# The residual of a decoder layer kept in its own column order, normalised in place, with the memory of a staging ring as a place of the weight stream

## The chip, the cores and the metric

The kernel runs on one core of a Trainium2 chip, as one launch. The metric is the device time of the execution in microseconds (us). The kernel before was run three times: 1680.66, 1681.29 and 1682.52 us, with a median of 1681.29.

## The reference, cut to what matters

One layer of a decoder with 256 tokens of 2048 channels, all in float32. Three attention branches are projected, gated and merged; then comes the part that the change touches, and a mixture of 32 experts:

```python
x = layer_norm(ALPHA * x + merged @ w_o, ln1_g, ln1_b)      # 256 x 2048
y = hier_moe(x, w_grp, b_grp, w_rt, b_rt, w1, w3, w2)
x = layer_norm(ALPHA * x + y, ln2_g, ln2_b)
# hier_moe: logits for 4 groups and 32 experts, best group, best two experts inside it;
#   hid = silu(xt @ w1[e]) * (xt @ w3[e])                   # 2048 -> 512
#   out = out + comb[:, e] * (hid @ w2[e])                  # 512 -> 2048, for each of the 32 experts
```

The three matrices of each expert are 4 MB each; all 32 experts are read, some 400 MB.

## The kernel before, in words

**Up to the output projection.** The projections run as a list of units. Each unit loads a piece of 128 x 512 floats of a weight matrix into a ring of six places (`stg`, six times 512 columns of the tile `stt`), splits it into a high and a low part (ScalarE casts, VectorE subtracts, line 155 and 156), and runs three matmuls for each half of the tokens (lines 215 to 217). The function `emit` issues a unit's load five units ahead and its split two units ahead. A place of the ring is free again when the split of what lay in it is done; the split parts have three buffers.

**The output projection and the residual.** `merged @ w_o` runs in two halves of its contraction, each over five column blocks (`WO`: three of 512, two of 256 columns); that is 32 units for each half. The residual lives in the tile `wx`, one 2048-column half for each half `c` of the tokens (`x1p`). `load_x` brings the columns of x for a block straight into it, after the units that `XL` names; `residual_sum` (line 472) adds the product out of PSUM; `row_stats` takes the sums for the first norm. The columns of a block lie in `wx` in another order than in the matrix: column `p * nj + j` of the block is column `p` of chunk `j` (the host gives x in that order), so that `logit_step` can transpose chunks of 128 adjacent columns (line 501) and multiply them with the router's weights (line 505).

**Routing.** The last block is ordered by hand. `last_steps` and `route_steps` are generators for token half 0 ("a", and the end of its sums) and half 1 ("b" its sums, "c" its routing), stepped in an order that is written out; `V` pins instructions to program order on their engine, everything else is placed by a planner that works with estimated costs. Steps: sums, mean and reciprocal deviation (a power on POOL), logits, best group (line 861 and 864 mask the others), best two experts, positions (`pos`, a matmul with a triangle of ones), and `S`, the matrix that selects tokens (line 881). In the same steps `normalise` writes the normalised residual into another place and order, `x1n`: half of it in the staging ring's tile `stt`, half in a tile of its own, partly on ScalarE (line 841), partly on POOL (line 843). After that `wx` is free and becomes a place of the stream. `keep_warm` issues matmuls whose result nobody uses.

**Experts.** For each group of four experts `gather` multiplies `x1n` with `S` (line 991), `gathered` applies the norm's gain and bias (lines 998 and 1001), and `hidden` runs the products with `w1` and `w3` (line 1030), with weights that the class `Stream` loads into ten places of 16 KB a partition: four that are free early (`wk`, `wkk`), four (`wg`) and half of `acc` during the output projection, `yb` after it, `wx` after the copy. A place is refilled when the product that reads it has given it back (`used`). The first units are loaded and given back in halves (`HALVES`): the first product gives the first half of four places back after four of its eight rows `j`. From the second group on the memory is given back by whole units.

**At the end** of the first groups `residual` (line 973) adds the normalised residual, with gain and bias, to the sum of the experts' outputs.

Of the kernel before, what the change touches and what calls it, by code (L numbers as in the profile page):

```python
# [8 lines left out]
F32 = mybir.dt.float32  # L9
# [9 lines left out]
P = 128  # L19
# [24 lines left out]
XL = (1, 5, 12, 18, 22)  # L44
KW = (6, 6)
# [4 lines left out]
def hybrid_trunk(ctx: ExitStack, tc: tile.TileContext, xp, xT, memT, w_mem_kv, w_in, gq, gkv, g_kidx, b_kidx,  # L50
# [18 lines left out]
    wb = ctx.enter_context(tc.tile_pool(name="wb", bufs=1))  # L69
    stt = wb.tile([P, 6 * 512], F32, name="stt")  # L70
# [40 lines left out]
    wsp = ph1.enter_context(tc.tile_pool(name="wsp", bufs=3, side="right"))  # L111
# [326 lines left out]

    def load_x(i):
        o, w, kt = WO[i]  # L440
        for c in range(2):
            nc.sync.dma_start(x1p[c][:, kt:kt + w // P], xp[c * P:(c + 1) * P, kt:kt + w // P, :])

    def wo_evac(i, half):
# [3 lines left out]
        def ev(ps, cs=(0, 1)):  # L448
# [10 lines left out]
            for c in cs:  # L459
                for k in range(kt, kt + nj, 2):  # L460
                    row_stats(c, k)
# [13 lines left out]
    def row_stats(c, k):  # L475
        return nc.vector.bn_stats(R["st"][:, c, k // 2, :], x1p[c][:, k:k + 2].rearrange("t j p -> t (j p)"))

    def last_steps(c, ps):
# [3 lines left out]
        V(row_stats(c, NKT - 2))  # L482
# [9 lines left out]
    def logit_step(i, c):  # L492
# [136 lines left out]
    def keep_warm(n, tag="pa"):  # L629

        t = pa.tile([P, P], F32, name="warm", tag=tag, bufs=1 if tag == "lg" else 3)
        for _ in range(n):
            nc.tensor.matmul(t, ones, ones, start=True, stop=True)

# [30 lines left out]
    class Stream:  # L665
# [5 lines left out]

        def __init__(self, first):
# [8 lines left out]
            if first:  # L681
                a, b, c = HALVES
                self.jobs = [(k, h) for k in u[:a] for h in range(2)] + [(k, None) for k in u[a:b]]
                self.jobs += [(k, h) for h in range(2) for k in u[b:c]] + [(k, None) for k in u[c:]]
            else:
                self.jobs = [(k, None) for k in u]
# [7 lines left out]
        def ready(self):  # L694
# [10 lines left out]
            return old is None or (old, 1 if h is None else h) in self.done  # L705
# [8 lines left out]
        def load_now(self):  # L714
            assert self.ready()
            k, half = self.jobs[self.i]
# [15 lines left out]
            sl = slice(0, W2D) if half is None else slice(half * D, (half + 1) * D)  # L732
            nc.sync.dma_start(t[:, sl], src[:, sl])

        def need(self, key):
            while key not in self.slot or any(j[0] == key for j in self.jobs[self.i:self.i + 8]):
                self.load()
            return self.slot[key][0]

        def used(self, keys, h=1):  # L740

            for k in keys:
# [3 lines left out]
                self.done |= {(k, 0), (k, h)}  # L746
# [47 lines left out]

    x1n = [[stt[:, o:o + 1024].rearrange("t (k p) -> t k p", p=P) for o in v] for v in ((0, 1024), (2048,))]
    x1p = [wx[:, c * D:(c + 1) * D].rearrange("t (k p) -> t k p", p=P) for c in range(2)]
# [25 lines left out]
    yb2 = yp_.tile([P, W2D], F32, name="yb")  # L822
    main.add([yb2], True)

# [5 lines left out]
    def normalise(c, s, eng):  # L830

        v = x1p[c][:, 4 * s:4 * s + 4]
        d = x1n[c][s // 2][:, :, 64 * (s % 2):64 * (s % 2) + 64]
        if s < 3:
            vd = [(v.rearrange("t j (p a) -> t a j p", a=2), d.rearrange("t (a j) p -> t a j p", a=2))]
        else:
            vd = [(v[:, 2 * h:2 * h + 2].rearrange("t j (p b) -> t b j p", b=4),
# [483 lines left out]
```

## Time and profile before

| what | value |
|---|---|
| three runs | 1680.66, 1681.29, 1682.52 us |
| the profiled execution | 1680.39 us |
| its span, first to last instruction | 1678.6 us |
| TensorE, VectorE, ScalarE busy | 87%, 37%, 27% of the span |
| output projection, half 1 of its contraction ends | 747 us |
| expert stage | 747 us to the end |

A profile is of one execution. A busy TensorE is not one at its peak, since matmuls are pipelined. Lines such as L991 are lines of the kernel before. PEld is TensorE's loading of the stationary operand, SPq the queue from which DMAs are issued. The granted clock (PEclk) is a share of 2.4 GHz.

### The profile page before, as it was taken

What the parts mean: (1) busy time and instruction counts of PE and PEld (TensorE: products, weight loads), DVE (VectorE), ACT (ScalarE), POOL (GpSimd) and SP (SyncE); (2) the same over time, 40 slices, a digit from 0 to 9 for tenths busy, and PEclk for the clock granted to TensorE, in tenths of its full rate; (3) what the DMA queues carried; (4) which work ended last, traced back from release to release, by engine and by line L of the source; (5) the groups of instructions that cost most, each with busy time, mean ns of one, the idle gap of its engine ahead of it and who ended that gap; (6) DMA issues with size and microseconds to landing.
All of it is one profiled execution on the core that took longest, in us unless ns stands there. A gap on an engine that the chain in (4) does not pass through costs nothing.

```text
span 1678.6 us, 20715 instructions
## 1 busy us (share of the span) xinstructions
PE 1458.4 (87%) x7984; PEld 878.5 (52%) x7984; DVE 615.0 (37%) x1165; ACT 456.0 (27%) x841; POOL 12.6 (1%) x24
## 2 busy tenths in 40 slices
PE   9999999999999999998976967967868768769758
PEld 8989988888878887883321322312312212213212
DVE  6656866566565676551120210200200101101005
ACT  5545455665545444441100000000000000000100
POOL 0000000000000000010000000000000000000000
PEclk9999999999999999999987987978978879879879
DMA  7766565555887558959999999999999999999996
GB/s 238 230 188 169 157 171 163 175 170 177 279 299 230 185 183 276 329 187 380 429 426 429 428 427 429 428 426 428 427 428 428 428 428 428 427 429 428 428 413 230
DMA packets 120203, 543.67 MB, mean 324 GB/s; under 512 B 13904, under 2 KB 28064, under 8 KB 94880
## 3 DMA queue, kind: packets, MB, share of 16 engines
q1 hardware_dynamic: 120096, 542.27, 84.5%
q8 instruction: 64, 1.05, 0.3%
q14 instruction: 43, 0.35, 0.1%
HBM read 540.10 MB, written 2.12 MB: 323 GB/s over the span
## 4 chain that ended last, share of the span: by engine, by line
PE 54%; DMA 42%; DVE 1%; issue 1%; ACT 1%; SPq 1%; POOL 0%; ACTq 0%; DVEq 0%; POOLq 0%
DMA wg<-in_w_dram 15%; DMA wk<-in_w_dram 15%; PE ps L216 10%; PE ps L217 9%; PE ps L215 9%; PE h L1030 9%; DMA wkk<-in_w_dram 5%; DMA wx<-in_w_dram 4%; PE yp L1113 3%; PE ps L210 3%; PE ps L207 3%; PE ps L209 3%; DMA stt<-in_w_gate_dram 1%; PE yp L1136 1%; DMA stt<-in_w_o_dram 1%
## 5 line engine op out<-in xcount | busy, mean ns | idle before, releaser
L156 DVE TENSOR_TENSOR wl<-stt,wh 128x512 fp32r<-128x512 f32 (+1 forms) x492 | 333.7, 684 | 238.7 <-ACT wh L155 237.4
L155 ACT CAST wh<-stt 128x512 fp32r<-128x512 f32 (+1 forms) x492 | 302.1, 616 | 315.0 <-PE ps L217 129.8
L1030 PE MATMUL h<-wg,xg 128*32 128x512 f32 x896 | 230.2, 703 | 74.3 <-DMA wg<-in_w_dram 74.2
L1030 PE MATMUL h<-wk,xg 128*32 128x512 f32 x704 | 200.8, 709 | 58.0 <-DMA wk<-in_w_dram 58.0
L215 PE MATMUL ps<-wh,xH 128*128 128x512 f32 (+2 forms) x512 | 198.1, 389 | 0.3 <-ACT wh L155 0.2
L216 PE MATMUL ps<-wl,xH 128*128 128x512 f32 (+2 forms) x512 | 195.3, 381 | 2.9 <-DVE wl L156 2.8
L217 PE MATMUL ps<-wh,xL 128*128 128x512 f32 (+2 forms) x512 | 194.8, 381 | 0.0
L1001 DVE TENSOR_SCALAR xg<-gp,g1n,b1n 128x128 f32<-128x128 f32 x56 | 22.9, 410 | 424.9 <-PE h L1030 373.6
L1030 PEld LDWEIGHTS h<-wg,xg 128*32 128x32 f32 x896 | 50.7, 126 | 190.0 <-DMA wg<-in_w_dram 101.9
L1030 PE MATMUL h<-wkk,xg 128*32 128x512 f32 x208 | 117.0, 718 | 18.2 <-DMA wkk<-in_w_dram 18.2
L1030 PE MATMUL h<-wx,xg 128*32 128x512 f32 x208 | 114.2, 703 | 12.1 <-DMA wx<-in_w_dram 12.1
L998 ACT ACTIVATE xg<-gp,b1n,g1n 128x128 f32<-128x128 f32 x56 | 25.6, 457 | 356.5 <-PE h L1030 252.5
L1030 PEld LDWEIGHTS h<-wk,xg 128*32 128x32 f32 x704 | 44.0, 127 | 144.1 <-DMA wk<-in_w_dram 81.2
L216 PEld LDWEIGHTS ps<-wl,xH 128*128 128x128 f32 x512 | 96.7, 189 | 22.6 <-DVE wl L156 5.4
L215 PEld LDWEIGHTS ps<-wh,xH 128*128 128x128 f32 x512 | 96.3, 189 | 18.3 <-ACT wh L155 1.6
L217 PEld LDWEIGHTS ps<-wh,xL 128*128 128x128 f32 x512 | 96.6, 189 | 17.4
L1113 PE MATMUL yp<-wg,yb 128*32 128x512 f32 x368 | 95.0, 595 | 6.8 <-DMA wg<-in_w_dram 6.8
L1113 PE MATMUL yp<-wk,yb 128*32 128x512 f32 x304 | 91.4, 596 | 7.0 <-DMA wk<-in_w_dram 7.0
L1039 DVE COPY yb<-yp 128x512 f32<-128x512 f32 x15 | 10.4, 691 | 189.9 <-PE yp L1113 173.0
L207 PE MATMUL ps<-xH,wh 128*128 128x256 f32 x256 | 73.3, 286 | 0.0
L210 PE MATMUL ps<-xH,wl 128*128 128x256 f32 x256 | 72.7, 284 | 0.2 <-DVE wl L156 0.2
L209 PE MATMUL ps<-xL,wh 128*128 128x256 f32 x256 | 72.6, 284 | 0.0
(322 smaller groups left out, 1991.9 us busy)
## 6 DMA issues: line engine op xcount, KB each, us to landing
wg<-in_w_dram SPq DMA_DIRECT2D x75, 2048.0 KB, 27.6
wk<-in_w_dram SPq DMA_DIRECT2D x57, 2048.0 KB, 28.2
stt<-in_w_gate_dram SPq DMA_DIRECT2D x192, 256.0 KB, 3.1
wx<-in_w_dram SPq DMA_DIRECT2D x20, 2048.0 KB, 27.1
wkk<-in_w_dram SPq DMA_DIRECT2D x18, 2048.0 KB, 30.2
stt<-in_w_in_dram SPq DMA_DIRECT2D x104, 256.0 KB, 3.0
stt<-in_w_o_dram SPq DMA_DIRECT2D x64, 256.0 KB, 5.8
wg<-in_w_dram SPq DMA_DIRECT2D x14, 1024.0 KB, 8.5
```

The costliest lines, as they stand in the source:

```text
L155: nc.scalar.copy(h, src)
L156: nc.vector.tensor_tensor(l, src, h.bitcast(F32), ALU.subtract)
L207: nc.tensor.matmul(o, hb, a.H(kt), start=st_ and b % 2 == 0, stop=False, skip_group_check=True)
L209: nc.tensor.matmul(o, hb, a.L(kt), start=False, stop=False, skip_group_check=True)
L210: nc.tensor.matmul(o, lb, a.H(kt), start=False, stop=sp_, skip_group_check=True)
L215: nc.tensor.matmul(o, ha, wh, start=st_, stop=False)
L216: nc.tensor.matmul(o, ha, wl, start=False, stop=False)
L217: nc.tensor.matmul(o, la, wh, start=False, stop=sp_)
L998: nc.scalar.activation(xg[:, kt], gp[:, j], AF.Identity, scale=g1n[:, kt:kt + 1], bias=b1n[:, kt:kt + 1])
L1001: nc.vector.tensor_scalar(xg[:, kt], gp[:, j], g1n[:, kt:kt + 1], b1n[:, kt:kt + 1], ALU.mult, ALU.add)
L1030: nc.tensor.matmul(h[32 * e:32 * e + 32, :], xg[:, 8 * c + j, 32 * e:32 * e + 32], wt[e][:, j, :], start=(c == 0 and j == 0), stop=(c == 1 ...
L1113: nc.tensor.matmul(yps[n][32 * e:32 * e + 32, :], hT[:, 2 * k + j, 32 * e:32 * e + 32], wt[e][:, j, n * 512:(n + 1) * 512], start=(k + j = ...
```

## The change

- The residual is kept in the columns' own order. x is loaded into the staging ring (two places for each block, one for each token half) and the first `residual_sum` reads it from there, turning its order; the second works on adjacent columns. The loads come after units 3, 11, 19, 23 and 27 in place of 1, 5, 12, 18 and 22.
- The transposes of `logit_step` and the gathers read the residual with a step (4 or 2 columns, and 8 columns).
- `normalise` works in place, in pieces of 512 columns, on ScalarE alone; `x1n` is gone. `wx` stays the residual's and is no place of the stream any more.
- The staging ring's tile and the split parts of weights lie side by side and are closed after the output projection. A new tile `wq` of 16 KB lies there and is a place of the stream; its load is issued right after that of `yb`.
- The four units that are loaded in halves are loaded in a quarter, a quarter and a half, and the first product runs as rows 0 to 1, 2 to 3 and 4 to 7, each giving back what it has read.
- Six places hold unused matmuls (6, 6, 6, 10, 4, 12) in place of two (6, 6), all into one tile.

```diff
-XL = (1, 5, 12, 18, 22)
-KW = (6, 6)
+XL = (3, 11, 19, 23, 27)
+KW = (6, 6, 6, 10, 4, 12)
...
-    wb = ctx.enter_context(tc.tile_pool(name="wb", bufs=1))
-    stt = wb.tile([P, 6 * 512], F32, name="stt")
...
-    wsp = ph1.enter_context(tc.tile_pool(name="wsp", bufs=3, side="right"))
+    wss = ExitStack()
+    wb = wss.enter_context(tc.tile_pool(name="wb", bufs=1, side="right"))
+    stt = wb.tile([P, 6 * 512], F32, name="stt")
+    wsp = wss.enter_context(tc.tile_pool(name="wsp", bufs=3, side="right"))
...
         for c in range(2):
-            nc.sync.dma_start(x1p[c][:, kt:kt + w // P], xp[c * P:(c + 1) * P, kt:kt + w // P, :])
+            XR[i, c] = st = stg()[:, :w].rearrange("t (j p) -> t j p", p=P)
+            nc.sync.dma_start(st, xp[c * P:(c + 1) * P, kt:kt + w // P, :])
...
-        a = x1p[c][:, kt:kt + nj]
-        return nc.vector.scalar_tensor_tensor(a, a, 1.0 if half else ALPHA,
-                                              ps[:, :w].rearrange("t (p j) -> t j p", j=nj), ALU.mult, ALU.add)
+        a = cols_of(i, c)
+        if half:
+            return nc.vector.scalar_tensor_tensor(a, a, 1.0, ps[:, :w], ALU.mult, ALU.add)
+        return nc.vector.scalar_tensor_tensor(a.rearrange("t (p j) -> t p j", j=nj),
+                                              XR.pop((i, c)).rearrange("t j p -> t p j"), ALPHA,
+                                              ps[:, :w].rearrange("t (p j) -> t p j", j=nj), ALU.mult, ALU.add)
...
-            nc.tensor.transpose(tp[:, j, :], x1p[c][:, kt + j, :], ident)
+            nc.tensor.transpose(tp[:, j, :], cols_of(i, c)[:, j::nj], ident)
         xt = R["xs"] if nj == 4 else R["xs"][:, 2 * c:2 * c + 2]
-        R["xc"] = nc.scalar.copy(xt[:, :nj], tp[:, :nj])
+        V(nc.scalar.copy(xt[:, :nj], tp[:, :nj]))
+        if between:
+            between()
...
-                self.jobs = [(k, h) for k in u[:a] for h in range(2)] + [(k, None) for k in u[a:b]]
-                self.jobs += [(k, h) for h in range(2) for k in u[b:c]] + [(k, None) for k in u[c:]]
+                self.jobs = [(k, h) for k in u[:a] for h in ((0, 2), (2, 4))] + [(k, (0, 4)) for k in u[a:b]]
+                self.jobs += [(k, h) for h in ((0, 1), (1, 2), (2, 4)) for k in u[b:c]] + [(k, (0, 4)) for k in u[c:]]
...
+    wss.close()
+    wqp = ctx.enter_context(tc.tile_pool(name="wqp", bufs=1, reuse_waits="tile"))
+    wq = wqp.tile([P, W2D], F32, name="wq")
     main.add([yb2], True)
+    main.add([wq])
...
-    def normalise(c, s, eng):
...
+    def normalise(c, *ks):
+
+        for k in ks:
+            v = x1p[c][:, 512 * k:512 * k + 512]
+            V(nc.scalar.activation(v, v, AF.Identity, scale=rs1[:, c:c + 1], bias=nb1[:, c:c + 1]))
...
-        for s, eng in ((0, "p"), (1, "a"), (2, "a"), (3, "p")) if c == 0 else ((0, "a"), (1, "p"), (2, "a"), (3, "p")):
-            normalise(c, s, eng)
+        normalise(c, *(range(4) if c else range(2)))
...
     main.load()
+    main.load()
...
-    keep_warm(KW[0])
-    logit_step(len(WO) - 1, 1)
+    warm = keep_warm(KW[0])
+    logit_step(len(WO) - 1, 1, lambda: keep_warm(KW[1], warm))
+    normalise(0, 2, 3)
+    keep_warm(KW[2], warm)
...
-    keep_warm(KW[1])
+    keep_warm(KW[3], warm)
     for k in "caca":
         next(steps[k])
-    main.add([wx])
-    main.load()
...
-                pin(nc.tensor.matmul(gp[:, j, :], x1n[c][k4 // 2][:, 4 * (k4 % 2) + j, :], S[:, c].rearrange("p e s -> p (e s)"),
+                pin(nc.tensor.matmul(gp[:, j, :], x1p[c][:, k4 // 2 * 1024 + k4 % 2 * 4 + j:(k4 // 2 + 1) * 1024:8], S[:, c].rearrange("p e s -> p (e s)"),
...
+            keep_warm(KW[4], warm)
             for _ in steps["c"]:
                 pass
+            keep_warm(KW[5], warm)
...
-                hidden(0, 0, "1", xg, h1, 0, 4)
+                hidden(0, 0, "1", xg, h1, 0, 2)
+                hidden(0, 0, "1", xg, h1, 2, 4)
```

## Rows read from the trace of the kernel before

**Rows 1.** The profile page: the GB/s line of the 40 slices (42 us each), and the shares of the chain that ended last, by engine.
```profile
GB/s 238 230 188 169 157 171 163 175 170 177 279 299 230 185 183 276 329 187 380 429 426 429 428 427 429 428 426 428 427 428 428 428 428 428 427 429 428 428 413 230
...
PE 54%; DMA 42%; DVE 1%; issue 1%; ACT 1%; SPq 1%; POOL 0%; ACTq 0%; DVEq 0%; POOLq 0%
```

**Rows 2.** The table of windows: us from the span's start, length, busy us (count) of PE, PEld, DVE, ACT and POOL, then the granted clock, the DMA share and GB/s.
```profile
733.00:747.00 14.00, 13.89 (x115) 13.11 (x114) 6.25 (x17) 4.97 (x10) 1.16 (x2) 1.00 0.01 2
747.00:748.00 1.00, 0.65 (x8) 0.32 (x5) 1.00 (x5) 0.86 (x2) 1.00 (x3) 1.00 0.40 82
748.00:749.00 1.00, 0.48 (x5) 0.40 (x4) 1.00 (x8) 0.37 (x1) 0.84 (x2) 1.00 1.04 197
747.00:765.00 18.00, 16.06 (x124) 11.25 (x125) 10.43 (x51) 6.81 (x13) 4.70 (x7) 0.81 0.73 262
750.00:755.00 5.00, 4.54 (x31) 4.32 (x28) 3.35 (x17) 3.14 (x4) 2.40 (x3) 0.50 1.00 380
759.00:763.00 4.00, 4.00 (x39) 1.62 (x32) 0.84 (x3) 1.26 (x3) 0.00 (x0) 1.00 0.09 31
763.00:766.00 3.00, 3.00 (x31) 1.06 (x34) 0.82 (x2) 0.92 (x2) 0.00 (x0) 1.00 0.92 289
765.00:1640.00 875.00, 669.27 (x3596) 217.50 (x3592) 107.64 (x183) 48.53 (x98) 0.00 (x0) 0.87 1.01 427
```

**Rows 3.** The timeline of the DMA issues (SPq) from 745 to 770 us: start, us of issuing, line, what is loaded, count.
```profile
746.97 0.34 SPq L733 DMA_DIRECT2D yb<-in_w_dram  x1
...
752.60 0.34 SPq L733 DMA_DIRECT2D wx<-in_w_dram  x1
762.24 1.28 SPq L733 DMA_DIRECT2D wk<-in_w_dram  x3
```

**Rows 4.** The timeline of TensorE from 746 to 768 us: start, us, line, output and operands, shapes, count, and in brackets what it waited for. A float32 matmul leaves two records.
```profile
746.78 0.51 PE L633 MATMUL warm<-ones 128*128 128x128 bf16 x6
...
751.21 3.75 PE L991 MATMUL g<-S,stt 128*128 128x128 f32 x16 [0.47 <-DVE S L881]
754.76 0.26 PE L875 MATMUL pos<-o,tri 128*128 128x32 bf16 x2
...
754.94 3.72 PE L991 MATMUL g<-S,stt 128*128 128x128 f32 x24
758.59 0.63 PE L1030 MATMUL h<-wk,xg 128*32 128x512 f32 x3
...
766.82 1.16 PE L991 MATMUL g<-S,stt 128*128 128x128 f32 x8
767.81 1.06 PE L991 MATMUL g<-S,x1n 128*128 128x128 f32 x8
```

**Rows 5.** The timelines of VectorE and of POOL in the same stretch.
```profile
748.81 0.19 DVE L864 SCALAR_TENSOR_TENSOR lgt<-gne,lgt 128x32 f32<-128x32 f32 x1
...
750.38 0.72 DVE L881 TENSOR_TENSOR S<-posm,io 128x128 f32<-128x128 f32 x1
...
752.00 0.61 DVE L864 SCALAR_TENSOR_TENSOR lgt<-gne,lgt 128x32 f32<-128x32 f32 x1
...
753.18 0.22 DVE L871 TENSOR_TENSOR o<-io,ei 128x64 bf16<-128x64 f32 x1
...
755.33 0.29 DVE L881 TENSOR_TENSOR S<-posm,io 128x128 f32<-128x128 f32 x1
...
750.17 0.80 POOL L843 TENSOR_SCALAR stt<-wx,rs,nb 128x512 f32<-128x512 f32 x1 [0.70 <-DVE nb L848]
750.95 1.62 POOL L843 TENSOR_SCALAR x1n<-wx,rs,nb 128x256 f32<-128x256 f32 x2
```

**Rows 6.** Loads of the stationary operand for transposes: L1096 reads columns 2 apart, L501 adjacent ones. First from the views of each line (ns min/median/max), then from the timeline (start, us, count).
```profile
L1096 PEld LDWEIGHTS ht<-ident,yb x32: 194/209/218, 800.4 to 1629.2; 128*128 128x128 f32 x32
...
L501 PEld LDWEIGHTS xt<-ident,wx x32: 138/140/144, 704.4 to 747.7; 128*128 128x128 f32 x32
...
800.39 0.55 PEld L1096 LDWEIGHTS ht<-ident,yb 128*128 128x128 f32 x4 [1.81 <-issue]
...
718.32 1.02 PEld L501 LDWEIGHTS xt<-ident,wx 128*128 128x128 f32 x8
```

**Rows 7.** The output projection: the landing times of its weight loads (line 186, issued from 640.8 to 729.8 us), the DMA issues of units 11 to 14, the window from 656 to 691 us, the casts of three units on ScalarE and after a wait of three more, and the first and the last residual sum of the first half on VectorE.
```profile
DMA to landing us min/median/max: 2.9/5.9/8.3
...
651.74 3.79 SPq L186 DMA_DIRECT2D stt<-in_w_o_dram  x4
...
656.00:691.00 35.00, 34.53 (x195) 29.80 (x194) 20.83 (x33) 14.94 (x24) 0.00 (x0) 1.00 1.02 373
...
653.82 0.62 ACT L155 CAST wh<-stt 128x512 fp32r<-128x512 f32 x1 [0.74 <-DVE wl L156]
655.18 0.62 ACT L155 CAST wh<-stt 128x512 fp32r<-128x512 f32 x1 [0.74 <-DVE wl L156]
656.54 0.62 ACT L155 CAST wh<-stt 128x512 fp32r<-128x512 f32 x1 [0.74 <-DVE wl L156]
659.93 1.98 ACT L155 CAST wh<-stt 128x512 fp32r<-128x512 f32 x3 [2.77 <-DMA stt<-in_w_o_dram]
...
656.44 1.28 DVE L472 SCALAR_TENSOR_TENSOR wx<-wx,ps 128x512 f32<-128x512 f32 x2
...
691.05 0.74 DVE L472 SCALAR_TENSOR_TENSOR wx<-wx,ps 128x256 f32<-128x256 f32 x2
```

More of the change, by code (lines that the diff above doesn't have):

```diff
@@ L459, in ev @@
             for c in cs:
-                for k in range(kt, kt + nj, 2):
-                    row_stats(c, k)
+                for k in range(0, nj, 2):
+                    row_stats(i, c, k // 2)
             for c in cs:
@@ L490, in last_steps, with logit_step @@
         yield
-    def logit_step(i, c):
+    def logit_step(i, c, between=None):
         o, w, kt = WO[i]
@@ L627, in emit, with keep_warm @@
                 step()
-    def keep_warm(n, tag="pa"):
-        t = pa.tile([P, P], F32, name="warm", tag=tag, bufs=1 if tag == "lg" else 3)
+    def keep_warm(n, t=None):
+        if t is None:
+            t = pa.tile([P, P], F32, name="warm", tag="pa")
         for _ in range(n):
             nc.tensor.matmul(t, ones, ones, start=True, stop=True)
+        return t
     def load_m(q):
@@ L682, in __init__ @@
                 a, b, c = HALVES
[L683 to L684 removed]
+                self.jobs = [(k, h) for k in u[:a] for h in ((0, 2), (2, 4))] + [(k, (0, 4)) for k in u[a:b]]
+                self.jobs += [(k, h) for h in ((0, 1), (1, 2), (2, 4)) for k in u[b:c]] + [(k, (0, 4)) for k in u[c:]]
             else:
[L686 removed]
+                self.jobs = [(k, (0, 4)) for k in u]
         def add(self, ts, once=False):
@@ L704, in ready @@
                 old = self.free[0][1]
-            return old is None or (old, 1 if h is None else h) in self.done
+            return old is None or (old, h[1] - 1) in self.done
         def load(self):
@@ L715, in load_now @@
             assert self.ready()
-            k, half = self.jobs[self.i]
+            k, part = self.jobs[self.i]
             self.i += 1
@@ L731, in load_now, with used @@
             src = w[4 * q + e, c * r:(c + 1) * r, :].rearrange("(p j) n -> p (j n)", p=P)
-            sl = slice(0, W2D) if half is None else slice(half * D, (half + 1) * D)
+            sl = slice(*(x * W2D // 4 for x in part))
             nc.sync.dma_start(t[:, sl], src[:, sl])
         def need(self, key):
-            while key not in self.slot or any(j[0] == key for j in self.jobs[self.i:self.i + 8]):
+            while key not in self.slot or any(j[0] == key for j in self.jobs[self.i:self.i + 12]):
                 self.load()
             return self.slot[key][0]
-        def used(self, keys, h=1):
+        def used(self, keys, n=4):
             for k in keys:
@@ L745, in used @@
                     self.free.append((t, k))
-                self.done |= {(k, 0), (k, h)}
+                self.done |= {(k, i) for i in range(n)}
             while self.i < len(self.jobs) and self.ready():
@@ L793, in hybrid_trunk @@
     wx = g16.tile([P, W2D], F32, name="wx")
-    x1n = [[stt[:, o:o + 1024].rearrange("t (k p) -> t k p", p=P) for o in v] for v in ((0, 1024), (2048,))]
-    x1p = [wx[:, c * D:(c + 1) * D].rearrange("t (k p) -> t k p", p=P) for c in range(2)]
+    x1p = [wx[:, c * D:(c + 1) * D] for c in range(2)]
     w2k = ctx.enter_context(tc.tile_pool(name="w2k", bufs=2, reuse_waits="tile"))
@@ L828, in hybrid_trunk @@
     gne = cs2.tile([P, 2, NG], F32, name="gne")
-    def normalise(c, s, eng):
[L832 to L837, printed above, removed]
-                   d[:, :, 32 * h:32 * h + 32].rearrange("t (b j) p -> t b j p", b=4)) for h in range(2)]
-        for v, d in vd:
-            if eng == "a":
-                V(nc.scalar.activation(d, v, AF.Identity, scale=rs1[:, c:c + 1], bias=nb1[:, c:c + 1]))
-            else:
-                V(nc.gpsimd.tensor_scalar(d, v, rs1[:, c:c + 1], nb1[:, c:c + 1], ALU.mult, ALU.add))
+    def normalise(c, *ks):
+        for k in ks:
+            v = x1p[c][:, 512 * k:512 * k + 512]
+            V(nc.scalar.activation(v, v, AF.Identity, scale=rs1[:, c:c + 1], bias=nb1[:, c:c + 1]))
     def route_steps(c):
@@ L899, in hybrid_trunk @@
     xgp = ctx.enter_context(tc.tile_pool(name="xgp", bufs=1, reuse_waits="tile"))
-    x1n[1].append(xgp.tile([P, 8, P], F32, name="x1n"))
     xg = xgp.tile([P, NKT, P], F32, name="xg")
@@ L1255, in hybrid_trunk @@
             more = Stream(False)
-            more.add([t for t in slots if t is not main.ln] + [wx])
+            more.add([t for t in slots if t is not main.ln] + [wq])
             moe_round(more, False)
```

16 lines of the change are left out of this document (9 added, 7 removed).

## The prediction, made before the change was run

> **What bounds the kernel now.** Read first the slices of the page: from about 765 us on the DMA engines move some 428 GB/s in every slice until the tail, while the slice before it holds a hole [rows 1]. The reader is to see two regimes: up to 747 us TensorE paces the kernel, and from 765 to 1640 us the stream of expert weights does, at 427 GB/s with the DMA share at 1.01 [rows 2]. In the second regime TensorE, VectorE and ScalarE can get slower or faster without any effect; the end moves only with the number of bytes that the stream has moved by a given time. So the second view is the table of windows around the change of regime. From 733 to 747 us the DMA engines stand still (2 GB/s), from 759 to 763 almost (31 GB/s), and in the 18 us from 747 to 765 they run at a mean of 262 GB/s [rows 2]. The third view, the issues of the DMA queue, tells why: at 746.97 the first load of the pause goes out (into yb, once the last matmul of the output projection has freed its memory), at 752.60 the second (into wx, once both halves of the residual were copied out of it), and at 762.24 the third, when the first half of the first expert product has given its slots back [rows 3]. The two loads are 4.19 MB (two tiles of 16 KB in each of 128 partitions), so nothing is left to move before that give-back. The fourth view, TensorE and VectorE from 746 to 767 us, is the chain from the last residual sum through the routing to that give-back [rows 4, 5]. Every us taken from it, or from the amount of work before the give-back, is a us off the end, until the hole is closed.
>
> **The change part by part.** All times below are of the profiled run, whose execution time is 1680.39 us for a span of 1678.6; the median of the three runs is 0.90 above it, and I carry that over.
>
> *Second load at once.* wq lies in the memory of the staging buffers and split weights; both are dead after the projection's last matmul, which also frees yb. Its issue should stand some 0.4 us behind the one at 746.97 instead of at 752.60. By itself this gains nothing at the end, since a hole follows either way; it moves the run-out forward. The queue starts slowly: 82 and 197 KB in the first two us [rows 2], 0.28 MB by 749. The other 3.91 MB at 427 GB/s last 9.2 us: run-out at 758.2 instead of 759 to 760.
>
> *Give-back in quarters.* The first product ran from 758.59 to 762.24, where the queue issued: 3.65 us for four rows j [rows 3, 4]. Two rows take half: 1.83 us sooner. Bytes flow 0.85 us after the issue (762.24, and the window from 763 at 289 GB/s) [rows 2, 3]. Four quarters are 2.1 MB, 4.9 us of transfer, and the next four come back 1.83 us later, so they carry the queue over to the half.
>
> *Normalising on ScalarE alone.* The POOL instructions go. While they ran, VectorE's building of S took 0.72 us against 0.29 later, and the masking of the logits 0.61 against 0.19 [rows 5]. I take both differences, 0.43 and 0.42, as the cost of that company. The first ends S of half 0 at 750.7 instead of 751.1; both together bring the choice of half 1 from 753.40 (753.18 and 0.22 long) to 752.55. ScalarE gets eight pieces of 512; the cast of a piece of that size takes 0.62 [rows 7], so the last is done by about 753, when nothing waits for it: the gathers of half 0 need the first two pieces alone, those of half 1 start after 753.
>
> *Keeping TensorE busy.* The gathers of half 0 took 3.55 us for 16 records (751.21 to 754.76), with the granted clock at 0.50, the lower of its two levels, in that stretch; TensorE had been busy for 0.65 and 0.48 of the two us from 747 on [rows 2, 4]. Eight records later, at the full clock, take 0.99 (766.82, next start 767.81), so 16 take 2.0. The change puts 6, 6, 10, 4 and 12 idle matmuls where TensorE waited; six take 0.51 us [rows 4]. I take the full clock to be kept. Another step goes with it: in the rows, eight gathers of a later group slipped in at 754.94 ahead of half 1's sixteen [rows 4]; the twelve idle matmuls (1.0 us) now stand in the gap between 754.76 and 755.62 in which they slipped in. Their excess over the gap and the four ahead of the position sums cost about 0.3 us.
>
> *The new chain.* Half 0 gathers from 750.8 to 752.8; the position sum of half 1 starts then; S of half 1 ends 0.86 later, as in the rows (754.76 to 755.62) [rows 4, 5], at 753.7; with 0.3 for idle matmuls and 2.0 for the gathers the product starts at 756.0 or a little before (758.59 before). First quarters back at 757.6, bytes at 758.5. The run-out is at 758.2, so 0.3 us of hole is left. By 765 the stream would have moved 0.28 MB and 16 us at 427 GB/s, 7.11 MB, against 4.72 MB (18 us at 262) [rows 2]: 2.39 MB or 5.6 us is the most that the hole can give, and less 0.3 it is **5.3 us**. What is late next is the stream itself.
>
> *Reading a tile in another order.* The transposes for the logits now load columns 4 (or 2) apart, the gathers columns 8 apart. The nearest row is a transpose with columns 2 apart: 209 ns of a load against 140 for adjacent ones, yet four in a row take 0.55 us and eight adjacent 1.02, so their spacing is the same [rows 6]. I take nothing, with an upper bound of 69 ns for each: 32 gather records on the chain (2.2 us) and 24 transposes in the stretch that TensorE paces (1.7 us). The Trainium skill says otherwise (Advanced Engine Details and Errata, Memory Cachelines): SBUF is read in lines of 16 bytes, and an access pattern that meets a new line with every element is penalised. With columns 2 apart two elements share a line, so the row does not refute it; 4 and 8 apart would meet it, and the sum by it is a rival below. No run here shows it yet.
>
> *The residual's loads through the staging ring.* x went straight into wx; now each pair takes two of the ring's six places, and holds them until its sum is made. A place's next load, and all behind it on SP's queue (projection weights and stream loads), waits for that. In the rows unit 13's load is the third of the four from 651.74 on, about 653.8; with this ring it can go out only after the sum that starts at 656.44, at 657.1. Its cast came third in the group from 659.93, at about 661.3 [rows 7]. A landing within 4.2 us costs nothing; landings took 2.9 to 8.3, median 5.9 [rows 7], which is 1.7 late at the median. Against that, the pairs come later than before (after units 3, 11, 19, 23, 27), so less is queued ahead of the weights, and a stall that is there now may go: a unit takes 1.36 us, 24 would take 32.6 from 656.44, and they took 34.6 to 691.05 [rows 7]. Bounds over five pairs: 2.0 gained to 20 lost. I take **1.0 lost**, a fifth of a us each, since with the pairs further apart I expect landings in the shorter half of these.
>
> *At nothing.* The sum in the columns' order, the contiguous products of the later residual, the in-place write and the swap of wx for wq as a slot (the count of slots stays) lie beside VectorE's idle time or in the regime that the DMA paces. If that cover were gone, the first-half sums at 0.4 us more each would cost some 4 us.
>
> Sum: 5.3 less 1.0 is 4.3 us. 1680.39 becomes 1676.1 in the profiled sense, and **1677.0** as a median.
>
> **Rivals.** *A: loads with a step.* Each strided load costs 69 ns more than an adjacent one. The gathers' 2.2 us move the resumption to 760.7, 2.4 ahead of 763.1; the transposes take 1.7, the ring 1.0: 1681.6, no change. For it speaks the longer load [rows 6], against it the equal spacing. *B: the clock falls all the same.* Half 0 takes its 3.55, S of half 1 ends at 755.2, its gathers take some 2.6 with the clock back midway, as in the rows; the product starts at 757.8, bytes at 760.5: 2.6 gained less 1.0, 1679.7. *C: the order does not come out.* Idle matmuls and the slipped-in gathers eat what the chain gains, and only the quarters are left: 1.8 less 1.0, 1680.5. *D: the ring starves the projection, and it is slower.* If four of the five pairs delay a weight by the median's 1.7 and one by the longest landing's 4.1, TensorE loses 10.9 us in the stretch that it paces: 1686.9. It decides from about 1.1 us for each pair on. For it speaks that the DMA engines are already full there (a share of 1.02 from 656 to 691) [rows 7], against it that the spacing of the pairs is wider.
>
> **How the numbers follow.** Forecast 0.47 (1674 to 1678.5), A 0.12, B 0.15, C 0.12, D 0.14. The range takes the forecast's best case (5.6 and the present stall of 2.0 gained: 1673.7) and reaches to the lower part of D: 1673.5 to 1685. About 0.2% (3.4 us) is what a measurement of this kernel can tell from no change. Faster by more: most of the forecast and a third of B, 0.48. Slower by more: most of D, 0.14. Within: 0.38.
>
> **What would show it.** Two stream loads behind each other at 747; quarter issues near 757.6 with the DMA share not falling below 0.9 between 749 and 765; the granted clock at 1.00 through 750 to 757; no POOL work but the two powers, and S at 0.3 us; gather records 0.12 us apart (A: 0.19). In the projection, the time from the first sum to the last matmul (656.44 to 746.97): 90.5 us if the ring costs nothing, 101 with D. The forecast is wrong if that stretch grows by more than 5 us, or if the issue of the first quarters is later than 760.

## The result and the profile after

| | kernel before | changed kernel |
|---|---|---|
| median of 5 runs each | 1681.29 us (1680.66 to 1682.52) | 1690.3 us (1689.43 to 1692.6) |
| ratio, 95% interval | | 1.0057 [1.0045, 1.0068] |
| profiled execution, span | 1680.39, 1678.6 us | 1690.3, 1688.5 us |
| last matmul of the projection done, issue into `yb` | 746.97 us | 755.31 us |
| from there to the first give-back | 15.27 us | 15.03 us |
| from there to the end of the span | 931.6 us | 933.2 us |

The change makes the kernel 0.57% slower, some 9 us. The last three rows split the 9.9 us between the two spans: 8.3 are lost before the expert stage begins, and the 1.6 behind it stand where 5.3 had been forecast as a gain.

The first view is again the page of the changed kernel. Each slice is 42 us. Against [rows 1] two neighbours differ most, the 16th and 17th, from 633 to 717 us: 257 and 296 GB/s, where the kernel before had 276 and 329. That is the output projection. The rate of the expert stream, 427 or 428 in nearly every slice, is unchanged.

```profile
GB/s 235 234 188 163 163 170 162 173 174 177 289 294 220 185 180 257 296 188 373 427 428 428 428 427 428 428 427 429 427 428 428 428 428 427 427 428 428 428 412 219
```

Where the first 8 us go is seen in the windows of the changed kernel (columns as in [rows 2]). The first row answers to the window of [rows 7]: TensorE had 195 records in these 35 us and now has 145, and the DMA engines moved 373 GB/s at a share of 1.02 and now move 303 at 0.89. Both have become less busy at once, so neither alone sets the pace here. In the second row, a part of the first, the granted clock is 0.70 on average, in a stretch where TensorE was busy for 3.13 of 5 us. The fall of the clock isn't what costs: e4 below has the same loads of x at a granted clock of 1.00 from 656 to 755 us, and its issue into `yb` comes as late (754.33).

```profile
656.00:691.00 35.00, 31.68 (x145) 25.05 (x145) 19.25 (x26) 13.00 (x21) 0.00 (x0) 0.95 0.89 303
685.00:690.00 5.00, 3.13 (x14) 2.93 (x15) 2.05 (x3) 1.94 (x4) 0.00 (x0) 0.70 0.64 202
...
755.00:770.00 15.00, 14.93 (x114) 13.30 (x117) 8.61 (x50) 8.59 (x15) 0.55 (x1) 1.00 0.72 283
...
767.00:771.00 4.00, 4.00 (x31) 2.10 (x34) 1.90 (x10) 1.72 (x4) 0.00 (x0) 1.00 0.05 17
```

The chain that ended last, from 650 to 705 us, says what the projection waits for: 59.4% of that stretch is the landing of `w_o` weights, where the same stretch of the kernel before has 28.1% (the last line). Pieces of 4 to 8 us lie along it, mostly with a cast and a subtract between them.

```profile
by line: DMA stt<-in_w_o_dram 59.4%; DVE wl L157 8.1%; ACT wh L156 6.9%; issue 6.8%; PE ps L217 6.7%; PE ps L218 6.1%; PE ps L216 5.4%; DVE wx L482 1.0%; ACTq L156 0.2%; DVEq L157 0.1%
...
651.04 6.62 DMA stt<-in_w_o_dram
...
661.02 7.31 DMA stt<-in_w_o_dram
...
678.96 6.92 DMA stt<-in_w_o_dram
...
by line: DMA stt<-in_w_o_dram 28.1%; PE ps L216 21.0%; PE ps L217 20.1%; PE ps L215 19.3%; DVE wl L156 3.8%; ACT wh L155 3.4%; SPq L442 2.7%; issue 1.0%; SPq L733 0.7%; PE xt L501 0.4%; ACTq L155 0.1%; SPq L186 0.0%
```

The next two views show why a weight is issued late: what the DMA queue waits for, from 640 to 705 us (us, times, longest), and its timeline. L446 loads x into the ring, L187 a weight; L482 is the sum that gives x's place back. Nine times in this stretch the queue stands for that sum, 8.9 us in all (5.3 and 3.6); in the kernel before it stood for a sum twice, 1.9 us in all. Behind the waiting instruction lie the weights of the next units and the stream's loads (L749 of the changed kernel).

```profile
SPq L446 <- DVE wx L482: 5.3, 4, 2.4
...
SPq L187 <- DVE wx L482: 3.6, 5, 1.4
```

```profile
661.50 1.08 SPq L446 DMA_DIRECT2D stt<-in_xp_dram  x2
663.61 3.09 SPq L187 DMA_DIRECT2D stt<-in_w_o_dram  x3
666.74 0.42 SPq L749 DMA_DIRECT2D wg<-in_w_dram  x1
669.80 3.54 SPq L187 DMA_DIRECT2D stt<-in_w_o_dram  x5
673.57 3.38 SPq L446 DMA_DIRECT2D stt<-in_xp_dram  x2
...
755.31 0.34 SPq L749 DMA_DIRECT2D yb<-in_w_dram  x1
755.89 0.34 SPq L749 DMA_DIRECT2D wq<-in_w_dram  x1
757.66 0.33 SPq L918 DMA_DIRECT2D xs<-in_ln_rows_dram  x1
770.34 1.28 SPq L749 DMA_DIRECT2D wk<-in_w_dram  x3
771.67 0.44 SPq L749 DMA_DIRECT2D wkk<-in_w_dram  x1
772.15 1.68 SPq L749 DMA_DIRECT2D wk<-in_w_dram  x3
```

After the projection the queue does what the forecast said: `yb` and `wq` go out within 0.6 us of each other. But the first quarter comes back 15.03 us later, where 10.6 had been forecast (757.6 less 746.97), and the window from 767 to 771 is a hole of 17 GB/s. TensorE's timeline has the reason; it answers to [rows 4]:

```profile
758.83 4.09 PE L997 MATMUL g<-S,wx 128*128 128x128 f32 x16
762.76 0.20 PE L883 MATMUL pos<-o,tri 128*128 128x32 bf16 x2
...
762.97 5.51 PE L997 MATMUL g<-S,wx 128*128 128x128 f32 x22
768.41 0.63 PE L1036 MATMUL h<-wk,xg 128*32 128x512 f32 x3
```

Sixteen gather records take 4.09 us with the granted clock at 1.00, longer than the 3.75 us that [rows 4] has for sixteen at a clock of 0.50. The views of the lines (ns min/median/max) show each load of the stationary operand at 336 ns for columns 8 apart, and 212 for the transposes, 4 or 2 apart, where [rows 6] has 140 for adjacent columns and 209 for 2 apart.

```profile
L997 PEld LDWEIGHTS g<-S,wx x64: 312/336/338, 758.8 to 781.7; 128*128 128x128 f32 x64
...
L512 PEld LDWEIGHTS xt<-ident,wx x32: 195/212/217, 712.9 to 756.0; 128*128 128x128 f32 x32
```

### The profile page after: what moved, and what is told of

The parts are those of the page before. It is cut to its first block, busy times and chain, and to the rows that moved or that the text cites. A ratio compares the mean times of both kernels' runs of the same rounds, so it can differ in the third digit from the quotient of the medians.

```text
span 1688.5 us, 20794 instructions
## 1 busy us (share of the span) xinstructions
PE 1503.2 (89%) x8016; PEld 937.4 (56%) x8016; DVE 613.0 (36%) x1165; ACT 458.4 (27%) x845; POOL 8.1 (0%) x18
## 4 chain that ended last, share of the span: by engine, by line
PE 56%; DMA 40%; DVE 1%; issue 1%; ACT 1%; SPq 1%; POOL 0%; ACTq 0%; DVEq 0%; POOLq 0%
DMA wg<-in_w_dram 15%; DMA wk<-in_w_dram 14%; PE ps L217 9%; PE ps L218 9%; PE ps L216 9%; PE h L1036 9%; PE yp L1122 4%; DMA wq<-in_w_dram 4%; DMA wkk<-in_w_dram 4%; PE ps L211 3%; PE ps L208 3%; PE ps L210 3%; DMA stt<-in_w_o_dram 2%; DMA stt<-in_w_gate_dram 1%; PE yp L1145 1%
## 5 line engine op out<-in xcount | busy, mean ns | idle before, releaser
L1004 ACT ACTIVATE xg<-gp,b1n,g1n 128x128 f32<-128x128 f32 x56 | 25.6, 457 | 380.0 <-PE h L1036 248.8
L1036 PE MATMUL h<-wq,xg 128*32 128x512 f32 x208 | 116.9, 717 | 9.2 <-DMA wq<-in_w_dram 9.2
L997 PE MATMUL gp<-S,wx 128*128 128x128 f32 x448 | 114.5, 417 | 9.0 <-DVE yb L1106 4.7
L997 PEld LDWEIGHTS gp<-S,wx 128*128 128x128 f32 x448 | 108.9, 335 | 23.3 <-issue 7.5
L217 PEld LDWEIGHTS ps<-wl,xH 128*128 128x128 f32 x512 | 96.4, 188 | 23.8 <-DVE wl L157 6.8
L1122 PE MATMUL yp<-wg,yb 128*32 128x512 f32 x368 | 89.4, 595 | 2.5 <-DMA wg<-in_w_dram 2.5
L1122 PE MATMUL yp<-wk,yb 128*32 128x512 f32 x304 | 86.9, 599 | 3.3 <-DMA wk<-in_w_dram 3.3
```

The costliest lines, as they stand in the source:

```text
L217: nc.tensor.matmul(o, ha, wl, start=False, stop=False)
L997: pin(nc.tensor.matmul(gp[:, j, :], x1p[c][:, k4 // 2 * 1024 + k4 % 2 * 4 + j:(k4 // 2 + 1) * 1024:8], S[:, c].rearrange("p e s -> p (e s) ...
L1004: nc.scalar.activation(xg[:, kt], gp[:, j], AF.Identity, scale=g1n[:, kt:kt + 1], bias=b1n[:, kt:kt + 1])
L1036: nc.tensor.matmul(h[32 * e:32 * e + 32, :], xg[:, 8 * c + j, 32 * e:32 * e + 32], wt[e][:, j, :], start=(c == 0 and j == 0), stop=(c == 1 ...
L1122: nc.tensor.matmul(yps[n][32 * e:32 * e + 32, :], hT[:, 2 * k + j, 32 * e:32 * e + 32], wt[e][:, j, n * 512:(n + 1) * 512], start=(k + j = ...
```

## The experiments

The kernels of one batch ran on one chip beside runs of the kernel before; the batches' medians of the kernel before lie between 1678.9 and 1681.3 us, so times are compared by ratio. In the table, *yb* is the issue into `yb` in the profiled execution, and the columns after it are counted from there: the first give-back, the moment by which the DMA transfers of the trace have moved 165 and 543 MB of the 543.7 (their bytes added up in order of their ends), and the end of the span.

| run | ratio, 95% interval | yb | give-back | 165 MB | 543 MB | end |
|---|---|---|---|---|---|---|
| before | 1 | 746.97 | 15.27 | 25.7 | 927.9 | 931.6 |
| changed | 1.0057 [1.0045, 1.0068] | 755.31 | 15.03 | 25.7 | 928.8 | 933.2 |
| e1, x not through the ring | 1.0012 [1.0003, 1.0020] | 745.69 | 15.01 | 26.0 | 928.5 | 932.9 |
| e2, before with the ring | 1.0057 [1.0042, 1.0071] | 755.61 | 15.26 | 25.6 | 927.6 | 931.4 |
| e3, before with the new places | 0.9998 [0.9989, 1.0006] | 743.16 | 14.12 | 24.5 | 927.0 | 930.7 |
| e4, adjacent gathers | 1.0047 [1.0033, 1.0060] | 754.33 | 10.26 | 21.5 | 923.8 | 928.3 |
| e5, e1 and e4 | 0.9979 [0.9970, 0.9987] | 745.16 | 10.27 | 22.0 | 925.0 | 929.4 |
| e6, before with quarters | 1.0004 [0.9996, 1.0013] | 746.35 | 13.26 | 23.8 | 927.1 | 931.1 |
| e7, e6 and idle matmuls | 1.0001 [0.9993, 1.0010] | 745.47 | 11.49 | 23.0 | 926.7 | 930.7 |
| e8, e7 and ScalarE alone | 0.9997 [0.9988, 1.0006] | 746.02 | 10.55 | 23.1 | 927.1 | 931.3 |
| e9, e5 with rows reordered | 0.9984 [0.9974, 0.9993] | 743.57 | 10.26 | 21.5 | 924.3 | 928.7 |
| e10, e9 with halves | 0.9984 [0.9975, 0.9993] | 744.19 | 11.97 | 22.4 | 924.4 | 928.6 |

Kernels before and e3 do the same in the expert stage and still differ by 1.2 us at 165 MB: that is how far one profile speaks.

### The ring: e1, e2, e3

e1 is the changed kernel with x loaded straight to where it is used, in its natural order, so that no place of the ring is held and the first sum turns nothing.

```diff
-            XR[i, c] = st = stg()[:, :w].rearrange("t (j p) -> t j p", p=P)
-            nc.sync.dma_start(st, xp[c * P:(c + 1) * P, kt:kt + w // P, :])
+            nc.sync.dma_start(cols_of(i, c).rearrange("t (j p) -> t j p", p=P), xp[c * P:(c + 1) * P, kt:kt + w // P, :])
...
+        return nc.vector.scalar_tensor_tensor(a, a, 1.0 if half else ALPHA, ps[:, :w], ALU.mult, ALU.add)
...
-        ("xp", perm(a["x"][0].T).transpose(2, 1, 0)), ...
+        ("xp", a["x"][0].reshape(T, NKT, P)), ...
```

> The changed kernel, with x in its natural column order loaded straight into wx (no place of the staging ring, no turned sum; the places of the loads, after units 3, 11, 19, 23 and 27, stay). Ring theory (the two ring places that each pair holds until its sum starve the projection): the loss of the first half of the projection goes, the stream's lag of some 9 us at 146 MB falls to about 0, and the time to 1680.5 to 1682.5 us. Rival, the later places of the loads: 1690, as the changed kernel. Rival, the turned sums (1.07 us against 0.68 on VectorE) hold up the splits: 1680.5 to 1682.5 too; the next kernel tells it from the ring.

e2 is the kernel before with x through the ring, and its own sums (0.68 us for 512 columns, where the turned ones of the changed kernel take 1.07).

```diff
-XL = (1, 5, 12, 18, 22)
+XL = (3, 11, 19, 23, 27)
...
-            nc.sync.dma_start(x1p[c][:, kt:kt + w // P], xp[c * P:(c + 1) * P, kt:kt + w // P, :])
+            XR[i, c] = st = stg()[:, :w].rearrange("t (j p) -> t j p", p=P)
+            nc.sync.dma_start(st, xp[c * P:(c + 1) * P, kt:kt + w // P, :])
...
-        return nc.vector.scalar_tensor_tensor(a, a, 1.0 if half else ALPHA,
+        return nc.vector.scalar_tensor_tensor(a, a if half else XR.pop((i, c)), 1.0 if half else ALPHA,
...
```

> The kernel before, with x loaded through the staging ring at the changed kernel's places (after units 3, 11, 19, 23, 27) and nothing else changed; the sum reads the ring in adjacent columns. Ring theory: about 8 to 9.5 us slower than before, 1689 to 1691. Rival, turned sums: 1681 to 1682, since no sum is turned here. Rival, later places: 1690.

e3 has the first of these edits, `XL`, alone.

> The kernel before, with the loads of x straight into wx as before, but after units 3, 11, 19, 23 and 27. Ring theory and turned sums: as before, 1680.5 to 1682 us. Rival, later places of the loads: 1689 to 1691.

The three ratios come out close to what the ring theory of the expectations says. Taken out of the changed kernel, the ring gives back 0.45%; put into the kernel before, it costs 0.57%; the places alone cost nothing. The issue into `yb` says it most plainly: in nine profiles without the ring it lies between 743.16 and 746.97, in the three with it between 754.33 and 755.61. The means are 745.2 and 755.1, so the ring costs some 9.9 us. The turned sums are not what costs, since e2 has none of them. The window of [rows 7] and the chain from 650 to 705 us in e2 look as in the changed kernel:

```profile
656.00:691.00 35.00, 29.90 (x139) 23.63 (x138) 16.52 (x25) 13.01 (x21) 0.00 (x0) 0.95 0.82 281
```

```profile
by line: DMA stt<-in_w_o_dram 61.7%; PE ps L216 8.6%; PE ps L217 7.6%; PE ps L215 6.9%; ACT wh L155 6.7%; DVE wl L156 5.4%; issue 2.7%; SPq L736 0.8%; SPq L186 0.8%; ACTq L155 0.3%; DVE wx L475 0.1%; DVEq L156 0.1%
```

and in e1 the same window has the records and the rate of the kernel before (its chain, with 41.5% of `w_o` landings, lies between the two, so that share alone doesn't give the price):

```profile
656.00:691.00 35.00, 34.21 (x195) 29.98 (x194) 20.66 (x35) 15.02 (x25) 0.00 (x0) 1.00 1.01 370
```

### The step: e4, e5

e4 is the changed kernel with gathers that read 128 adjacent columns; e5 is e1 with the same edit. Both leave out the match of these columns with the rows of `w1` and `w3`, so they compute something else; e9 below puts the match back.

```diff
-  ... x1p[c][:, k4 // 2 * 1024 + k4 % 2 * 4 + j:(k4 // 2 + 1) * 1024:8], ...
+  ... x1p[c][:, (4 * k4 + j) * P:(4 * k4 + j + 1) * P], ...
```

> The changed kernel, with gathers that read 128 adjacent columns in place of columns 8 apart, so they bring other columns than the product's weights belong to (the computation is changed in that). Theory, stepped loads of the stationary operand cost twice (335 against 190 ns each, 0.24 us a record against 0.12) and pace the chain to the first give-back: the first quarters go out about 4 us earlier, the hole of some 4 us in the DMA after 767 us closes, and the time falls by 3.5 to 4.5 us to 1686 to 1687. Rival, something else paces that chain: 1690.

> The changed kernel without both suspects: x straight into wx and gathers that read adjacent columns (other columns than the weights belong to; the computation is changed in that). If the two suspects are all that stood between the forecast and the result, the forecast's chain is left: first quarters given back some 10.7 us after the last matmul of the projection, no hole left in the DMA, and 3.5 to 5.5 us less than the kernel before (1674 to 1676 against 1679.5). Rival, something else of the change costs too (the idle matmuls in the chain, the transposes with a step): within 2 us of the kernel before.

The timeline of TensorE in e4, and under it the view of the line (ns min/median/max), stand beside those of the changed kernel above: the same records take half the time, and the load falls from 336 to 192 ns.

```profile
757.85 2.05 PE L997 MATMUL g<-S,wx 128*128 128x128 f32 x16
...
759.95 2.77 PE L997 MATMUL g<-S,wx 128*128 128x128 f32 x22
```

```profile
L997 PEld LDWEIGHTS g<-S,wx x64: 186/192/192, 757.8 to 772.8; 128*128 128x128 f32 x64
```

The two groups are 2.04 and 2.74 us shorter, 4.78 in all, and the give-back comes 4.77 us sooner (15.03 to 10.26): that is the whole of it. At the end of the span, counted from `yb`, 4.9 us of it arrive in e4 and 3.5 in e5. The ratios give 0.10% between the changed kernel and e4 and 0.33% between e1 and e5; the first is within its intervals, the second is not. So the time of e4 alone doesn't show the step (its fall was expected at 3.5 to 4.5 us, and the ratios have 1.7); the trace of e4 and the time of e5 do. With neither cost, e5 is faster than the kernel before by 0.21% [0.13, 0.30].

### The gains alone: e6, e7, e8

These put the parts that were meant to shorten the pause into the kernel before, one on top of the other. e6 has the quarters.

```diff
...
-                self.jobs += [(k, h) for h in range(2) for k in u[b:c]] + [(k, None) for k in u[c:]]
+                self.jobs += [(k, h) for h in ((0, 1), (1, 2), (2, 4)) for k in u[b:c]] + [(k, (0, 4)) for k in u[c:]]
...
-                hidden(0, 0, "1", xg, h1, 0, 4)
+                hidden(0, 0, "1", xg, h1, 0, 2)
+                hidden(0, 0, "1", xg, h1, 2, 4)
```

> The kernel before with one part of the change alone: the four units given back in a quarter, a quarter and a half, and the first product in rows 0 to 1, 2 to 3, 4 to 7. Theory: the first give-back comes 1.8 us sooner and so does the end, 1677.5 to 1678 against 1679.5. Rival, more and smaller transfers cost as much as they bring: 1679.5 or more.

e7 adds the six places of idle matmuls; the four places that the cut leaves out stand as in the changed kernel.

```diff
-KW = (6, 6)
+KW = (6, 6, 6, 10, 4, 12)
...
+            keep_warm(KW[4], warm)
             for _ in steps["c"]:
                 pass
+            keep_warm(KW[5], warm)
```

> The kernel before with the quarters and the six places of idle matmuls; normalising, gathers (adjacent columns) and the loads of x stay as before. Theory: granted clock 1.00 through the first gathers, 16 records in 2.0 us instead of 3.6, no later gathers slipped in ahead of half 1; the give-back comes 4 to 5 us sooner, the hole closes but for the late load into wx, and the time is 3 to 4.5 us under the kernel before: 1675 to 1676.5. Rival, the clock falls all the same or the idle matmuls stand in the way: as the quarters alone, 1677.5 to 1678.5.

e8 leaves the copy of the residual to ScalarE.

```diff
-        for s, eng in ((0, "p"), (1, "a"), (2, "a"), (3, "p")) if c == 0 else ((0, "a"), (1, "p"), (2, "a"), (3, "p")):
-            normalise(c, s, eng)
+        for s in range(2 + 2 * c):
+            normalise(c, s, "a")
...
+    normalise(0, 2, "a")
+    normalise(0, 3, "a")
```

> As the kernel before it in this list, with the copy normalised by ScalarE alone, none on POOL. Theory: the two long VectorE instructions (0.72 and 0.61 us) fall to 0.3 and 0.2, the give-back comes another 0.5 to 0.9 us sooner, and the time changes by less than 1 us either way, since wx is given to the stream later (eight pieces of 0.85 us in a row) and the hole is nearly closed already. Rival, POOL's company cost nothing on the chain: the give-back stays.

Each does in the trace nearly what was said of it. The give-back comes 2.0, 3.8 and 4.7 us sooner (in e7 4 to 5 had been expected). In e7 the gathers of half 0 run at the full clock, as their line shows beside the 3.75 us of [rows 4]:

```profile
749.74 2.02 PE L997 MATMUL g<-S,stt 128*128 128x128 f32 x16 [0.48 <-POOL stt L848]
```

And none moves the time by what a dozen runs of each can tell: 1.0004, 1.0001, 0.9997. The times that were expected of e6 and e7, 1.5 to 2 and 3 to 4.5 us less, did not come. The stream is 1.9 to 2.7 us ahead at 165 MB, still 1.6 to 2.6 at 530 MB, 0.8 to 1.2 at 543 MB and 0.3 to 0.9 at the end of the span. The second load still waits for the copy (753.54 in e8, three us before the give-back), so a sooner give-back finds most of that load still to be moved; that this is why 4.7 us become 2.5 is argued, not tried.

### Both costs taken out: e9, e10

e9 computes the reference with the instructions of e5: the host gives the rows of `w1` and `w3` in the order in which adjacent columns select them, and the gain and bias of the norm to match.

```diff
+    def rows(v):
+        return v.reshape(-1, 2, 8, P, v.shape[-1]).transpose(0, 1, 3, 2, 4).reshape(v.shape)
...
-        ... ("w1", a["w1"][0]), ("w3", a["w3"][0]),
+        ... ("w1", rows(a["w1"][0])), ("w3", rows(a["w3"][0])),
...
```

> The kernel of e5 with the computation of the reference restored: the host gives the rows of w1 and w3 in another order inside each 1024 (row j*128+p where row p*8+j stood), and the first norm's gain and bias to match, so that gathers of 128 adjacent columns select the right values. No instruction of the chip's changes its shape and no transfer its size. Theory (the loss of the change is the ring plus the stepped stationary loads, and both can be had back without leaving work out): as e5, 1676.2 us, ratio 0.9979 against the kernel before, first give-back 10.3 us after the issue of yb. Rival (e5 was faster because wrong values went through its experts, by some effect of the data): not below 1679, ratio 1.000.

e10 has the four units in halves again.

> e9 with the four units in halves again, as in the kernel before, in place of quarters; the first product gives back after rows 0 to 3. Theory (the sooner start by quarters is taken back by pieces that move at 330 to 400 GB/s at a full DMA share, and by the end of the span, as the run of the kernel before with quarters alone showed): first give-back some 1.5 to 2 us later than in e9, hole longer by as much, but the pieces behind it at over 410 GB/s, and the end within 0.7 us of e9: 1675.5 to 1677. Rival (the quarters' 1.8 us reach the end once the ring and the steps are gone): 1678.

Both are faster than the kernel before by 0.16%, which is 2.7 us by the ratio of the runs: e9 with a median of 1675.8 us against 1678.9 beside it (11 and 21 runs), e10 with 1675.77. The interval of e9, 0.07 to 0.26%, reaches the 0.21% of e5. What e5 and e9 have beyond e8 is above all the second load, issued right behind that into `yb`; e8, with the same shorter chain but the late load, gains nothing that its runs can tell (0.9997, where e5 has 0.9979 and the intervals don't meet). So the early load is probably what lets the other parts count, though the prediction gave it nothing by itself; it was not put into the kernel before alone. The quarters give memory back 1.7 us sooner (10.26 against 11.97), are 0.9 us ahead at 165 MB, and equal at the end. The windows show one half of why. e9 first, then e10; the last two columns are DMA share and GB/s:

```profile
749.00:754.00 5.00, 5.00 (x51) 3.45 (x52) 3.37 (x17) 3.67 (x7) 0.00 (x0) 1.00 1.02 428
754.00:759.00 5.00, 5.00 (x50) 2.18 (x46) 0.82 (x2) 0.92 (x2) 0.00 (x0) 1.00 0.95 370
759.00:764.00 5.00, 5.00 (x48) 2.62 (x44) 1.15 (x3) 0.63 (x2) 0.00 (x0) 1.00 1.00 374
```

```profile
754.00:757.00 3.00, 3.00 (x29) 1.31 (x21) 0.10 (x1) 0.46 (x1) 0.00 (x0) 1.00 0.62 255
757.00:759.00 2.00, 2.00 (x21) 0.82 (x23) 0.82 (x2) 0.57 (x2) 0.00 (x0) 1.00 0.91 252
759.00:763.00 4.00, 4.00 (x40) 2.31 (x36) 0.00 (x0) 0.34 (x1) 0.00 (x0) 1.00 1.01 424
```

e10 has a hole near 757 that e9 has not, and then moves its 1 MB pieces at 424 GB/s, while e9's pieces of 0.5 MB fill the engines' time at 370 to 374. From 744 to 765 us the two average 374 and 347 GB/s, 0.57 MB or 1.3 us of stream apart; 0.6 of that is e9's earlier issue into `yb`, so less than half of the 1.7 us is left.

The Trainium skill (DMA: Bandwidth & Descriptors, Measured) advises batching transfers to 1 MiB or more; its figures are for transfers issued from GpSimd. The 0.5 MB pieces here, issued from SP, agree in direction: 370 to 374 against 424 GB/s, 12 to 13% less.

## Why the prediction was wrong

**Which step failed.** Two terms, both at places where the prediction had an upper bound and took a value near the lower one. The forecast was 1677.0; the changed kernel takes 1690.3, outside the range, on the other side of no change. Both signs that the prediction named came: the stretch from the first sum to the issue into `yb` grew by 8.5 us, and the first quarters went out at 770.34.

**The ring: mis-sized.** "I take 1.0 lost" for five pairs; the runs show 9.9 by the issue into `yb`, 0.45 to 0.59% or 7.6 to 9.9 us by ratios (e1 against the changed kernel, e2 against e3). Rival D had the mechanism and the size (10.9 us, 1686.9), with a chance of 0.14. Its test in the prediction was the stretch from the first sum to the last matmul, 101 us against 90.5: from 656.26, the start of the first sum, to 755.31 it is 99.0. The reason for the small value was that the pairs are spaced wider and hold less up in front of the weights. e3 shows the spacing to be free, but it doesn't help the ring. The argument counted each pair as one delay of one weight; the queue stands nine times for a sum, not five, and the loads of x wait for each other's sums too. A pair takes two of six places from its issue until its sum, 8 us (661.50 to 669.69) and more; meanwhile the weights have four places with landings that the trace of before put at 5.9 us [rows 7], and all later loads queue behind. Rival D counted five weights as well, so that its size came out is partly luck. The DMA share of 1.02 that was there before [rows 7] was the sign that no slack stood against this. What is shown is the price of holding the places. That it is the number of places left, and not the order on the queue alone, was not tried by itself.

**The step: taken at nothing.** "Their spacing is the same" was true of columns 2 apart and was carried to 8 apart. The gathers cost 4.78 us on the chain. The upper bound, 69 ns for each of 32 records, 2.2 us, was too small as well: the records are 0.25 us apart in place of 0.125, and there are 38 of them. Rival A had the mechanism, and half of its size. For the transposes the value of nothing held: eight loads 4 columns apart take 1.16 us, beside 1.02 for adjacent ones [rows 6], and e1, which has them, ends its projection at 745.69, among the kernels without them (743.16 to 746.97). The row is from the timeline of TensorE's loads in the changed kernel:

```profile
712.90 1.16 PEld L512 LDWEIGHTS xt<-ident,wx 128*128 128x128 f32 x8
```

The Trainium skill's rule (Advanced Engine Details and Errata, Memory Cachelines), weighed in the prediction, says that an access pattern with a new line of 16 bytes at each element is penalised. Columns 8 apart agree, with 336 ns against 192; columns 4 apart also meet a new line each time by that figure, and with 212 ns they don't differ from columns 2 apart at 209, so the size of a line that it gives isn't borne out by these loads. No gather with columns 4 apart and no transpose with columns 8 apart was run.

**The chain and the hole: right in kind, too large.** With both costs out, the give-back comes 10.26 us after the issue into `yb`; the prediction had 10.6. The steps inside were right as well: the two loads at once, the clock (1.00 from 755 to 770, so rival B is out), S at 0.28 us and the masking at 0.18 to 0.19 with no POOL work but the two powers. VectorE's timeline of the changed kernel answers to [rows 5]:

```profile
756.85 0.18 DVE L872 SCALAR_TENSOR_TENSOR lgt<-gne,lgt 128x32 f32<-128x32 f32 x1
...
758.50 0.28 DVE L889 TENSOR_TENSOR S<-posm,io 128x128 f32<-128x128 f32 x1
...
763.30 0.28 DVE L889 TENSOR_TENSOR S<-posm,io 128x128 f32<-128x128 f32 x1
```

But of the 5.3 us that this was to be worth, 4.2 and 3.7 are there at 165 MB (e9, e5) and 2.9 and 2.2 at the end of the span. The prediction's premise that every us taken from the chain is a us off the end isn't borne out by e6 to e8, whose give-back came 2.0 to 4.7 us sooner and whose end, counted from `yb`, 0.3 to 0.9. The first loss is the rate of the small pieces: ten us at some 372 in place of 427 GB/s are 1.3 us, for which the prediction had no term. The rest goes in the last 50 us: at 530 MB the lead is still 4.1 and 3.7. One profile of each kernel doesn't settle what takes it, and it stays open. Of rival C the records that slipped in are there (22 in place of 16), yet the chain kept its length: in e4 this group starts at 759.95, while S of half 1 is built until 760.55, so the slipped-in records fill a wait.

**The edits at nothing.** The turned sums take 1.07 us, 0.39 more than the 0.68 of the others, about the 0.4 that the prediction named; e2 has the whole loss without them, so no cost of theirs can be seen. The normalisation's last run of pieces on ScalarE ended 5.8 us after the issue into `yb` (756.80 and 4.34 long, in the row of ScalarE's timeline below), where the prediction had 6, and nothing waited for it.

```profile
756.80 4.34 ACT L852 ACTIVATE wx<-wx,nb,rs 128x512 f32<-128x512 f32 x6
```

**The sum by measured terms** in the profiled executions: 8.3 for the ring, 4.9 for the step and −3.3 for the rest (e4's end less that of before) are 9.9 us, the difference of the spans. The sum closes by construction, since its last term is a remainder; what was measured apart is the ring (9.9 by the means of `yb`) and the step.

## What to carry to other kernels

A place in a staging ring costs by how long it is held: before routing another tensor through a ring that a saturated stretch depends on, count the places left for its own traffic against the landing time, and don't price it as one late transfer. A price measured at one step of an access pattern need not hold at another: here the trace had the step 2 and the change the step 8, and even the upper bound drawn from it was half of the cost, so such a step is to be timed first. And when several gains are added up, time each alone: here those that were put into the kernel before showed in the trace and not in the time, and the two costs, 8.3 and 4.9 us, took four times the 3.3 that the gains were worth.

## What the runs showed of the hardware

- Loading a stationary operand of 128 x 128 floats at a granted clock of 1.00: 140 ns in a transpose with adjacent columns, 209 and 212 with columns 2 and 4 apart; in a gather 192 adjacent and 336 with columns 8 apart. Of these patterns only the one with columns 8 apart moved the matmuls far apart, from 0.125 to 0.25 us; eight transposes in a row took 1.16 us with columns 4 apart and 1.02 adjacent.
- The stream moves pieces of 2 MB at 427 GB/s, of 1 MB at 424 and of 0.5 MB at 370 to 374, all with the engines' time filled (share 0.95 to 1.02).
- Streams that were 1.9 to 2.7 us ahead at 165 MB ended 0.3 to 0.9 us ahead (e6 to e8 against before, counted from `yb`): the gain in the pause reached the end only in part.
